# Order of the first loads, of the Gates' first products and of the background steps in a one-core hybrid mLSTM and gating layer

## The chip, the core and the metric

The kernel runs on one core of one Trainium2 chip. The metric is the device time of one execution in microseconds (us), as the median of several runs. The engines are TensorE (PE in the profile; PEld is its weight load), VectorE (DVE), ScalarE (ACT), GpSimd (POOL) and the queue of SyncE (SP), which here issues all DMAs.

## The reference

One layer over 1024 latent tokens and 256 context tokens of width 1024, in float32. What matters here is the feed-forward part, which stands twice in the layer for the latent tokens and once for the context, and the conditioning, which gives each of its shifts, scales and gates:

```python
mods = jnp.split(jax.nn.silu(c) @ w_ada[layer] + b_ada[layer], N_MOD, axis=-1)
mods_c = jnp.split(jax.nn.silu(c_ctx)[None] @ w_ada[layer] + b_ada[layer], N_MOD, axis=-1)

def ffn_sublayer(h, shift, scale, gate, g, w_in, w_out):
    hn = modulate(rmsnorm(h, g), shift, scale)
    a, b = jnp.split(hn @ w_in, 2, axis=-1)
    y = (jax.nn.silu(a) * b) @ w_out
    return h + 0.5 * gate[:, None, :] * y
```

`w_in` is 1024 x 5632, `w_out` 2816 x 1024. Between the two feed-forward parts lie the projections, a bidirectional mLSTM scan and a spatial gating, which the change does not touch.

## The kernel before

**Arithmetic.** Matrices are multiplied in pairs of float32r pages: `split` (L144, L145) copies a page on ScalarE into its high part and subtracts it on VectorE for the low part; three matmuls (high x high, high x low, low x high) make one product of a 128 x 128 block with 512 columns. The large products use seven block products in place of eight, in the manner of Strassen and Winograd: weights and activations are first added and subtracted in blocks. These block products are numbered 1 to 7. Product 1 and 2 need only the first token half's pages (`fa`), 5 and 6 the pages `fb`, 7, 4 and 3 the pages `fc`.

**Stages, in order.** (1) Prologue: four quarters of the first two conditioning vectors, as matmuls of `w_ada` pages of 256 KB (`ada_pages`, `ada_mm`, L803; tiles `adapg`, `adr`), the context's sum of squares (`Norm.sq`, `rstd`, `bcast`) and its normalised pages `hnc` (`mod0`). (2) The context's first feed-forward product, `pa` and `pb`, with weights loaded by `Weights`. (3) `A.gate` and (4) `A.outp`: the latent tokens' feed-forward. (5) The context's output, the projections, the scan, the merge. (6) `B.gate` and `B.outp`, the second feed-forward part.

**A Gate.** `Gate` walks over 22 weight rows `f`, paired as `kp` and `kp + 11`, each with products 1 to 7 of twelve matmuls (L381). The order is a list, `steps`. The first three `f` (0, 11, 1), the head, go side by side: product 1 of all three, product 2 of all three, and so on in the order `HSEQ`; all other `f` go one by one in the order `SEQ` = (1, 6, 5, 7, 2, 4, 3). Weights are loaded, combined (`presum` and `load`, on GpSimd, L347 to L365) and split `depth` products ahead into pages of a ring; `depth` is 4 and becomes larger at the first product 3, when the stage's input is given back and the pool `rg` is opened in its place. Results come together in banks A (products 1 and 2), B (6, 7, 4) and C (5, 3), so that VectorE must have read bank B after product 6 (`u1`, L401) before product 7 may add to it, and again after product 7 (`y2`, L404) before product 4. The pool for small pages "t2" has 12 slots, "fx" 12 as well; the raw rows of the head (`rawh`, two for each `f`) and their sums (`s1s`, two halves in a page) lie in "fx", loaded ahead by `preload`; other rows come into four slots `rawq`.

**Factors.** The pages of the second token half's combinations are made while the Gate runs: `Factors.late` gives a list of small items (in `B.gate` after `rstd`, some empty items, `bcast`, and with a normalisation `inplace` for each page). They go into the queue `todo`; `pump`, called after each three matmuls or so, pays 512 of credit, and an item costs 512 unless it says otherwise. An item that is due is taken out at once (`while not F.ready(p)`).

**Background.** A generator computes three more conditioning vectors on VectorE: 25 steps each, of which step 24 and 25 (`ada_fin`) use a small PSUM bank and end in `mods` (L758). It takes one step at each `tick`: in `A.gate` at each fourth product after number 36, in `A.outp` after each row of products other than 4 and 7.

**Order on an engine.** The framework lays out each engine's instructions by its own model of time, with the program's order as the priority. An engine can thus start a later piece of work where an earlier one is not ready in that model; on the chip each engine then runs its list in order.

## Time and profile before

| | us |
|---|---|
| median of 3 runs (lowest, highest) | 2702.27 (2700.63, 2704.98) |
| the profiled execution | 2708.92 |
| its span, first to last instruction | 2707.1 |
| TensorE busy | 2660.7 |
| VectorE busy | 1966.9 |
| ScalarE busy | 1081.5 |
| GpSimd busy | 447.6 |

The profile is of one execution. "Busy" counts each engine's own instructions; matmuls are pipelined and their ends are modelled, so that a matmul row lasts 0.39 us though the next one may start 0.23 us after it. Rows in order of time begin with start and duration; brackets at their end hold the idle time just before and what ended it. Rows by group hold the count, the busy time in us and the mean in ns.

### The profile page before, as it was taken

Reading aid. Unit: us, or ns where it says so; the run is one execution under the profiler, and the core shown is the slowest. Engines: PE = TensorE matmul, PEld = TensorE weight load, DVE = VectorE, ACT = ScalarE, POOL = GpSimd, SP = SyncE. Lnnn points to the kernel's source line nnn. Section 1 sums busy time; section 2 is a strip of 40 time slices with the busy share of each in tenths; the row PEclk is TensorE's granted clock in tenths of the full one; section 3 lists DMA queues with packets and bytes.
Section 4 is the critical chain, followed back from the end, with each engine's and each line's share of the span. In section 5 each row is a group of like instructions: output and inputs, shape, how many; then the busy total and the mean of one; then the engine's idle time right before and its main releaser. Section 6 shows DMA issues by size and latency. Waiting matters only on the chain.

```text
span 2707.1 us, 35713 instructions
## 1 busy us (share of the span) xinstructions
PE 2660.7 (98%) x12754; PEld 2211.7 (82%) x12754; DVE 1966.9 (73%) x3379; ACT 1081.5 (40%) x1840; POOL 447.6 (17%) x422
## 2 busy tenths in 40 slices
PE   9999999999999999999999999999999999999998
PEld 5987888887889878888888888888887788888887
DVE  4898777777979647788774878677568766666755
ACT  4663333334337525554443342112255333333432
POOL 0042323210000120000002005442102332320000
PEclk9999999999999999999999999999999999999999
DMA  8843344448588322246653477548140333337555
GB/s 297 309 172 117 121 152 140 137 163 309 186 262 273 110 78 85 105 142 215 192 164 113 142 236 260 168 164 283 57 158 20 130 138 124 106 125 262 201 159 171
DMA packets 202401, 456.74 MB, mean 169 GB/s; under 512 B 20592, under 2 KB 54640, under 8 KB 202224
## 3 DMA queue, kind: packets, MB, share of 16 engines
q1 hardware_dynamic: 202224, 454.47, 49.8%
q8 instruction: 100, 1.64, 0.3%
q14 instruction: 77, 0.63, 0.1%
HBM read 328.95 MB, written 125.51 MB: 168 GB/s over the span
## 4 chain that ended last, share of the span: by engine, by line
PE 73%; DVE 14%; DMA 5%; issue 4%; ACT 2%; POOL 1%; SPq 1%; POOLq 0%; DVEq 0%; ACTq 0%
PE pq L1232 14%; PE qb L381 13%; PE po L500 12%; PE pt L1700 9%; PE qa L381 7%; PE pr L1151 6%; DVE ring L145 2%; PE pc L1022 2%; PE pn L1813 2%; PE pu L1540 2%; DVE adacc L743 1%; DMA adapg<-in_w_ada_dram 1%; PE pkc L1212 1%; DMA graw<-fsp 1%; ACT ring L144 1%
## 5 line engine op out<-in xcount | busy, mean ns | idle before, releaser
L144 ACT CAST ring<-rawq 128x512 fp32r<-128x512 f32 x432 | 266.5, 621 | 569.3 <-PE qb L381 186.3
L145 DVE TENSOR_TENSOR ring<-rawq,ring 128x512 fp32r<-128x512 f32 x432 | 317.1, 738 | 159.7 <-ACT ring L144 158.2
L500 PE MATMUL po<-gring,wring 128*128 128x512 f32 (+1 forms) x1896 | 426.2, 385 | 3.7 <-DVE mods L758 2.8
L500 PEld LDWEIGHTS po<-gring,wring 128*128 128x128 f32 x1896 | 349.2, 188 | 76.5 <-issue 4.7
L381 PE MATMUL qb<-fc,ring 128*128 128x512 f32 x1440 | 344.6, 393 | 10.9 <-DVE y L404 5.6
L381 PEld LDWEIGHTS qb<-fc,ring 128*128 128x128 f32 x1440 | 271.4, 189 | 73.8 <-DVE u L401 10.0
L381 PE MATMUL qa<-fa,ring 128*128 128x512 f32 x1056 | 253.9, 390 | 1.2 <-DVE ring L145 0.7
L381 PEld LDWEIGHTS qa<-fa,ring 128*128 128x128 f32 x1056 | 197.7, 188 | 43.4 <-ACT ring L144 1.2
L381 PE MATMUL qb<-fb,ring 128*128 128x512 f32 x984 | 229.8, 389 | 0.0
L381 PEld LDWEIGHTS qb<-fb,ring 128*128 128x128 f32 x984 | 184.6, 188 | 38.7 <-DVE fb L145 0.3
L1232 PE MATMUL pq<-fc,ring 128*128 128x512 f32 x864 | 212.8, 394 | 0.5 <-DVE py L1245 0.4
L1232 PEld LDWEIGHTS pq<-fc,ring 128*128 128x128 f32 x864 | 160.8, 188 | 35.8 <-DVE py L1245 1.9
L144 ACT CAST wring<-rw 128x512 fp32r<-128x512 f32 x154 | 96.0, 623 | 224.8 <-PE po L500 196.5
L1700 PE MATMUL pt<-yp,ring 128*128 128x512 f32 x768 | 184.2, 396 | 0.0
L1700 PEld LDWEIGHTS pt<-yp,ring 128*128 128x128 f32 x768 | 144.1, 188 | 29.3
L145 DVE TENSOR_TENSOR wring<-rw,wring 128x512 fp32r<-128x512 f32 x154 | 106.1, 689 | 76.6 <-ACT wring L144 76.4
L1232 PE MATMUL pq<-fa,ring 128*128 128x512 f32 x576 | 142.3, 395 | 0.0
L1232 PE MATMUL pq<-fb,ring 128*128 128x512 f32 x576 | 137.6, 393 | 0.0
L1232 PEld LDWEIGHTS pq<-fa,ring 128*128 128x128 f32 x576 | 108.4, 190 | 23.1 <-DVE ring L145 0.2
L1232 PEld LDWEIGHTS pq<-fb,ring 128*128 128x128 f32 x576 | 107.6, 188 | 22.8 <-PE pu L1581 0.4
L743 DVE SCALAR_TENSOR_TENSOR adacc<-adapg,sc,adacc 128x512 f32<-128x512 f32 x140 | 107.3, 783 | 16.6 <-DMA adapg<-in_w_ada_dram 15.7
L144 ACT CAST ring<-rawt 128x512 fp32r<-128x512 f32 x64 | 39.6, 621 | 183.9 <-PE pt L1700 178.2
(343 smaller groups left out, 4342.1 us busy)
## 6 DMA issues: line engine op xcount, KB each, us to landing
adapg<-in_w_ada_dram SPq DMA_DIRECT2D x144, 256.0 KB, 3.6
fsp<-fhl SPq DMA_DIRECT2D x66, 512.0 KB, 2.7
gring<-fsp SPq DMA_DIRECT2D x66, 512.0 KB, 3.8
raw<-in_w1i_dram SPq DMA_DIRECT2D x44, 512.0 KB, 5.9
graw<-fsp SPq DMA_DIRECT2D x88, 256.0 KB, 3.0
rawq<-in_w1i_dram SPq DMA_DIRECT2D x38, 512.0 KB, 4.0
rawq<-in_w2i_dram SPq DMA_DIRECT2D x38, 512.0 KB, 3.3
fsp<-x SPq DMA_DIRECT2D x66, 256.0 KB, 2.8
```

The lines of the kernel that those rows point to most:

```text
L144: S.copy(hl[:, 0, :], src)
L145: V.tensor_sub(hl[:, 1, :], src, hl[:, 0, :].bitcast(F32))
L381: T.matmul(pt, hl[:, x, sl], pages[p][k][:, y, :], start=first and i == 0, stop=i == 11, skip_group_check=not first)
L500: T.matmul(pt[:, cs], w[:, x, sl], g[:, y, cs], start=grp and kp == 0 and i == 0, stop=kp == NFP - 1 and i == 2, skip_group_check=not grp)
L743: eng.scalar_tensor_tensor(acc, pgt, sc2[:, q, k:k + 1], acc, ALU.mult, ALU.add)
L1022: T.matmul(pt, hl[d // 4][:, x, sl], g[:, y, :], start=f == 0 and d % 2 == 0 and i == 0, stop=f == NF - 1 and i == 2, skip_group_check=True)
L1151: T.matmul(self.pt[m], pg[:, x, sl], hl[:, y, :], start=first and k == 0 and i == 0, stop=k == 3 and i == 2, skip_group_check=not first)
L1212: T.matmul(self.cp[:, o:o + 256], hl[:, x, k * 128:(k + 1) * 128], hnc[kc][:, y, :], start=p == 1 and k == 0 and i == 0, stop=p in (2, 4) ...
L1232: T.matmul(pt, hl[:, x, k * 128:(k + 1) * 128], pg[k][:, y, :], start=first and k == 0 and i == 0, stop=k == 3 and i == 2, skip_group_chec ...
L1540: T.matmul(pu[:, 0:257], ksl[:, kt * 128:(kt + 1) * 128], wv, start=True, stop=True)
L1700: T.matmul(pt, hl[:, x, k * 128:(k + 1) * 128], pg[:, y, :], start=kh + k + i == 0, stop=kh == 1 and k == 3 and i == 2)
L1813: T.matmul(pn[:, 0:257], qi[:, c_, :], self.C[d][:, c_, :], start=False, stop=c_ == 1)
```

## The change

Three parts. The prologue loads the second quarter's `w_ada` pages ahead of the context, and the context in two DMAs of four pages instead of eight of one; the context's `rstd` moves into the middle of the third quarter's products. The Gate's head has four `f`: products 1 and 2 of the first pair, products 1 and 2 of the second pair, then 5, 6, 7, 4, 3 of the first pair side by side, then 6, 5, 7, 4, 3 of each of the second pair by itself. Only the first pair's raw rows and sums lie in "fx"; the second pair's come through `rawq` and a slot of "t2". Items of `todo` in the Gate cost 640 instead of 512, with two more empty ones before `bcast` in the second. The background takes a step at each third product after number 42 and none in the last four rows of product 2.

```diff
--- before.py
+++ after.py
@@ -148,6 +148,14 @@
 
     def nop():
         pass
+
+    def it(f, *args):
+        return lambda: f(*args)
+
+    def slow(fn, *args, cost=1024):
+        f = it(fn, *args)
+        f.cost = cost
+        todo.append(f)
 
     credit = [0]
 
@@ -312,7 +320,7 @@
             return res
 
     SEQ = (1, 6, 5, 7, 2, 4, 3)
-    HSEQ = (1, 2, 5, 6, 7, 4, 3)
+    HSEQ = (5, 6, 7, 4, 3)
 
     class Gate:
 
@@ -321,7 +329,10 @@
             self.name, self.raw, self.ring, self.depth, self.sums, self.pairs = name, raw, ring, depth, sums, pairs
             fs = [f for kp in range(pairs) for f in (kp, kp + pairs)]
             self.head = fs[:head]
-            self.steps = [(f, p) for p in HSEQ for f in self.head] + [(f, p) for f in fs[head:] for p in SEQ]
+            two = [self.head[o:o + 2] for o in range(0, head, 2)]
+            self.steps = [(f, p) for fs_ in two for p in (1, 2) for f in fs_] + [(f, p) for p in HSEQ for f in two[0]]
+            self.steps += [(f, p) for fs_ in two[1:] for f in fs_ for p in SEQ if p > 2]
+            self.steps += [(f, p) for f in fs[head:] for p in SEQ]
             self.order = deque(self.steps)
             self.ready = deque()
             self.held = 0
@@ -508,7 +519,7 @@
                     for m, pt in enumerate(pts):
                         tile_(pt, kp, m, w, g)
                     self.fill()
-                    if tick is not None and p not in (4, 7):
+                    if tick is not None and p not in (4, 7) and not (p == 2 and kp > 6):
                         tick()
                 for hx in range(halves if p == 3 else 0):
                     cs = slice(hx * 512 // halves, (hx + 1) * 512 // halves)
@@ -522,7 +533,7 @@
             last()
 
     HLP = (3, 5, 6)
-    HEAD = 3
+    HEAD = 4
     warm = cp.tile([128, 1], F32, name="warm")
 
     fx = pool("fx", side="right")
@@ -561,11 +572,11 @@
             self.q = None
 
         def head(self):
-            s1s = [fxpage("s1s", F32) for _ in range(2)]
-            s1v = deque(pg[:, i, :] for pg in s1s for i in range(2))
+            s1s = fxpage("s1s", F32)
+            s1v = deque(s1s[:, i, :] for i in range(2))
             self.q = Gate(self.w_in, lambda f: fxpage("rawh", F32, (128, 1024)), self.ring, 4,
-                          lambda n: s1v.popleft(), NFP, HEAD)
-            self.heads = [(f, i) for i in (0, 1) for f in self.q.head]
+                          lambda n: s1v.popleft() if s1v else t2(n), NFP, HEAD)
+            self.heads = [(f, i) for i in (0, 1) for f in self.q.head[:2]]
 
         def preload(self):
             if self.heads:
@@ -598,7 +609,8 @@
             q, F = self.q, self.F
             q.raw = lambda f: xpage("raw", "rawq")
             q.fill()
-            todo.extend(items)
+            for fn in items:
+                slow(fn, cost=640)
             for n, (f, p) in enumerate(q.steps):
                 while not F.ready(p):
                     todo.popleft()()
@@ -610,7 +622,7 @@
                     q.sums = lambda n: self.rg.tile([128, 512], F32, name=n, tag="sums", bufs=2)
                     q.mid = lambda: self.rg.tile([128, 512], F32, name="ft", tag="ft", bufs=1)
                 q.step(f, p, F.pages, self.store)
-                if tick is not None and n % 4 == 0 and n > 36:
+                if tick is not None and n % 3 == 0 and n > 42:
                     tick()
             flush()
 
@@ -797,9 +809,11 @@
             pages.append(pg)
         return pages
 
-    def ada_mm(pages):
+    def ada_mm(pages, mid=None):
         pr = sm_ps("adr")
         for k in range(NKT):
+            if k == 4 and mid is not None:
+                mid()
             T.matmul(pr[0:2, 0:2 * QW], sc2[:, :, k], pages[k // KP][:, k % KP].rearrange("p m c -> p (m c)"),
                      start=k == 0, stop=k == NKT - 1)
         return pr
@@ -827,9 +841,6 @@
     def half_gate(i, m, q):
         V.tensor_scalar(hgate[:, i, q, :], mods[:, m, q, :], 0.5, None, ALU.mult)
 
-    def it(f, *args):
-        return lambda: f(*args)
-
     gcsp = dr.tile([NFP, 2, 128, 2, 256], F32, name="gcsp")
     W = Weights([("w1i", f, 1024) for f in range(2 * NF)], "w1")
     A = Stage("1", "w1i", 3)
@@ -838,9 +849,9 @@
     hc = [hcp[d // 4][:, d % 4, :] for d in range(NKT)]
     pos = fxpage("pos", F32, (128, 320))
 
-    def load_c(hc):
-        for d in range(NKT):
-            nc.sync.dma_start(hc[d], a["cT"][d])
+    def load_c(hcp, n):
+        for i, pg in enumerate(hcp):
+            nc.sync.dma_start(pg, a["cT"][i * n:(i + 1) * n].rearrange("d p t -> p d t"))
 
     def add_pos(tb, d):
         hv = h[tb][d].rearrange("p (r c) -> p r c", c=64)
@@ -855,9 +866,9 @@
     for _ in range(10):
         T.matmul(junk[:, 0:128], ones, ones, start=True, stop=True)
     apg = [ada_pages(0)]
-    load_c(hc)
-    for qt in (1, 2, 3):
-        apg.append(ada_pages(qt))
+    apg.append(ada_pages(1))
+    load_c(hcp, 4)
+    apg += [ada_pages(2), ada_pages(3)]
     nc.sync.dma_start(cst[:, 1:], a["cst"].rearrange("p (a b) -> p a b", a=5)[:, 1:])
     nc.sync.dma_start(pos, a["pos"])
     hncp = [fxpage("hnc", F32R, (128, 2, 2, 256)) for _ in range(4)]
@@ -871,11 +882,10 @@
     for d in range(NKT):
         nct.sq(d)
     prs.append(ada_mm(apg[1]))
-    nct.rstd()
     for qt in range(NQ):
         ada_out(qt, prs[qt])
         if qt < 2:
-            prs.append(ada_mm(apg[qt + 2]))
+            prs.append(ada_mm(apg[qt + 2], None if qt else nct.rstd))
         if qt == 0:
             nct.bcast()
         if qt:
@@ -885,11 +895,6 @@
 
     n1 = [Norm(h[tb], 512, V) for tb in range(2)]
     s0, b0 = smod[:, 0, 0, :], mods[:, 0, 0, :]
-
-    def slow(fn, *args, cost=1024):
-        f = it(fn, *args)
-        f.cost = cost
-        todo.append(f)
 
     for f in range(NF):
         if f < NKT:
@@ -1009,7 +1014,7 @@
 
     hcp = [t2("hc", F32, (128, 2, 256)) for _ in range(4)]
     hc = [hcp[d // 2][:, d % 2, :] for d in range(NKT)]
-    load_c(hc)
+    load_c(hcp, 2)
     pcs = [mm_ps("pc") for _ in range(4)]
     wload(2)
     wsplit(1)
@@ -1956,7 +1961,7 @@
                     todo.append(lambda k=k, p=p: B.F.early(fpage, p, k))
     flush()
     n1_ = n3[1]
-    B.gate([n1_.rstd] + [nop] * 3 + [n1_.bcast] + B.F.late(fpage, lambda k: [lambda: n1_.inplace(k, m7, m6)]))
+    B.gate([n1_.rstd] + [nop] * 5 + [n1_.bcast] + B.F.late(fpage, lambda k: [lambda: n1_.inplace(k, m7, m6)]))
 
     def put(n_, tb, d, pool_, cs=slice(0, 512)):
         o_ = n_.h[d]
```

## The prediction

> **What bounds the kernel now.** I read the page first, then the waits of TensorE, then its order of time in the places that the waits name, then VectorE in the same stretches.
>
> ```profile
> span 2707.1 us, 35713 instructions
> PE 2660.7 (98%) x12754; PEld 2211.7 (82%) x12754; DVE 1966.9 (73%) x3379; ACT 1081.5 (40%) x1840; POOL 447.6 (17%) x422
> ...
> PE qb L381 <- DVE y L404: 5.6, 4, 2.7
> PE qb L381 <- DVE u L401: 5.4, 11, 2.4
> PE qa L381 <- DVE u L401: 4.0, 2, 2.6
> PE adr L803 <- DMA adapg<-in_w_ada_dram: 3.8, 3, 2.4
> PE rb L215 <- DVE diag L211: 2.9, 2, 1.8
> PE po L500 <- DVE mods L758: 2.8, 2, 2.3
> ```
>
> TensorE is busy for 98% of the span, so only its idle time can be won, 46.4 us in all by this row, and a little more that hides in slow matmuls. The waits (total, times, longest) lie where the change works: the Gate's products (L381, three rows, 15.0 us), the first products of the prologue (L803) and the first output stage (L500). Not one matmul is added or removed.
>
> The second Gate, in TensorE's order of time (start, duration, then in brackets the idle time and its releaser):
>
> ```profile
> 2041.69 2.43 PE L381 MATMUL qa<-fa,ring 128*128 128x512 f32 x10
> ...
> 2049.11 1.10 PE L215 MATMUL rb<-diag,ones 128*128 128x512 f32 x2 [1.11 <-DVE diag L211]
> ...
> 2079.57 3.00 PE L381 MATMUL qa<-fc,ring 128*128 128x512 f32 x12 [1.47 <-DVE u L401]
> 2085.14 15.51 PE L381 MATMUL qa<-fc,ring 128*128 128x512 f32 x60 [2.57 <-DVE u L401]
> 2100.49 8.32 PE L381 MATMUL qb<-fc,ring 128*128 128x512 f32 x36
> 2108.65 2.88 PE L381 MATMUL qa<-fa,ring 128*128 128x512 f32 x12
> ...
> 2116.81 0.61 PE L381 MATMUL qa<-fa,ring 128*128 128x512 f32 x2
> 2119.82 4.61 PE L381 MATMUL qb<-fc,ring 128*128 128x512 f32 x12 [2.39 <-DVE u L401]
> ...
> 2126.55 5.60 PE L381 MATMUL qb<-fc,ring 128*128 128x512 f32 x24
> ```
>
> 36 matmuls from 2100.49 to 2108.65 are three products: 2.72 us for a product of twelve. The head's 21 products should take 57.1 and take 2108.65 - 2041.69 = 67.0: 9.8 lost, of which about 1.5 are the Norm's own small matmuls (`rb` at 2049.11 and the sums ahead of it). The next five products (13.6) take 17.9: 4.3 lost. After the two longest waits matmuls run slowly: 60 took 15.51 where 13.8 is due, 12 took 4.61 where 2.9 is. A long wait costs about 1.7 on top of itself. So 12.6 us can be won here.
>
> The reason is VectorE (a window with busy us of PE, PEld, DVE, ACT, POOL; the groups of that window; its order of time, with GpSimd's):
>
> ```profile
> 2050.00:2109.00 59.00, 54.96 (x233) 44.38 (x232) 56.48 (x84) 33.55 (x56) 11.13 (x6) 0.97 0.04 14
> ...
> L293 DVE TENSOR_TENSOR h<-h 128x512 f32<-128x512 f32 x16 | 13.1, 852 | 0.0
> L145 DVE TENSOR_TENSOR fc<-h,fc 128x512 fp32r<-128x512 f32 x12 | 8.7, 729 | 0.0
> L246 DVE SCALAR_TENSOR_TENSOR h<-h,smod,rb 128x512 f32<-128x512 f32 x8 | 5.8, 742 | 1.3 <-PE rb L215 1.3
> ...
> 2080.43 3.46 DVE L293 TENSOR_TENSOR h<-h 128x512 f32<-128x512 f32 x2
> 2084.41 0.68 DVE L401 TENSOR_TENSOR u<-p,qa 128x512 f32<-128x512 f32 x1
> 2085.01 0.68 DVE L145 TENSOR_TENSOR ring<-rawh,ring 128x512 fp32r<-128x512 f32 x1
> ...
> 2079.92 3.42 POOL L348 TENSOR_TENSOR rawq<-rawq 128x512 f32<-128x512 f32 x2
> ```
>
> It is busy for 56.5 of 59 us. Operations start 0.60 apart (2084.41, 2085.01). The product at 2085.14 starts when the `u` add of 2084.41 is done, and that add stood behind two subtractions that took 3.46, not some 1.3, while GpSimd worked on 2079.92 to 2083.34.
>
> **The change part by part.**
>
> *Heads of the Gates.* Twelve products of different data now run ahead of product 7, as before, but eight of them (not six) need only the pages that stand since the start. The dues, counted in products from the head's start, go for product 5, 6, 7, 4, 3 from 6, 9, 12, 15, 18 to 8, 10, 12, 14, 16. VectorE's work for these pages: 8 `inplace` (some 0.66 apart), 16 subtractions, 20 splits, 5.3 + 36 x 0.60 = 26.9, from 2050 on. Up to product 7: 19.7 of it, nine ring splits 5.4, two `u` adds 1.2 (three before): 26.3, with 2 lost to GpSimd ends at 2078.3; TensorE is there at 2041.7 + 32.6 + 2 = 2076.3. Wait: 2.0. Then two products (5.4) against pages of product 4 (4.8), two ring splits (1.2), three adds (1.8): 2.4 more. Then 5.4 against 2.4 + 1.2 + 3.6: 1.8 more. What helps beyond this count is room: s1s and rawh take 5 of 12 "fx" slots and not 8, so the pages of products 4 and 3 need not wait for raw rows to be used up. After the first pair ten products (27.2) stand against ten ring splits, fourteen adds, eight operations of `out`: 32 x 0.60 = 19.2, covered; without that cover the next wait is the fifth matrix's first product, whose banks free last. Left: 6.2 and something for the adjacency below, 6.6 of 12.6. **Gain 6.0**, ends -3 and 12.6.
>
> The third and fourth matrix's GpSimd sums (two operations each) move into the gate; GpSimd's two at 2079.92 cost VectorE 3.46 - 1.3 = 2.1. That is in the 2 us above; at the worst, both on the path, 2 x 2.1. [...]
>
> *Product 4 right behind product 7* in the second pair: product 4 accumulates in the bank that the `y` add (L404) must read first; elsewhere product 2 stands between. Two places in each Gate. Bounds: nothing, if TensorE takes other work (at 2116.81 it started two matmuls of product 2 ahead of product 7, so the order on the engine is filled by what is ready); 0.68 for the add and some 0.2 each way when VectorE is free; 2.7, the longest wait in the row on `y`, when it isn't. Queued behind it: all later products. I take 0.9 for each, half of them filled: 0.4 in the second Gate (above) and 0.9 in the first.
>
> *First Gate.* Same order, without `inplace`:
>
> ```profile
> 239.25 2.88 PE L381 MATMUL qa<-fa,ring 128*128 128x512 f32 x12
> ...
> 255.68 7.38 PE L381 MATMUL qb<-fc,ring 128*128 128x512 f32 x24 [2.67 <-DVE y L404]
> 262.89 2.88 PE L381 MATMUL qa<-fa,ring 128*128 128x512 f32 x12
> ...
> 283.19 2.88 PE L381 MATMUL qa<-fa,ring 128*128 128x512 f32 x12
> ...
> 239.00:263.00 24.00, 21.33 (x87) 17.15 (x86) 22.33 (x33) 8.89 (x16) 8.75 (x5) 0.93 0.53 168
> ```
>
> Seven products from 239.25 to 262.89: 23.6 for 19.0, 4.6 lost; seven more to 283.19: 20.3, 1.3 lost. VectorE is busy 22.33 of 24 there, with what three matrices that end together leave behind. Two and two spread this. I take 1.2 left and 0.9 for the adjacency: **gain 3.8**, ends -3 (all four waits as long as the row's) and 5.9.
>
> The Gate's item rate (cost 640 for 512) puts one item on 1.25 slots: 51 items are done by slot 64, product 16; product 3's page is due just there, so the rate itself adds nothing while VectorE is the bound. The two more empty items let `bcast` fall later than `diag`; the wait on `diag` in the second head (1.11) is inside the 12.6.
>
> *Background.* It advances every third product from 45 and not every fourth from 40: 37 steps for 29. Each is two operations:
>
> ```profile
> L743 DVE SCALAR_TENSOR_TENSOR adacc<-adapg,sc,adacc 128x512 f32<-128x512 f32 x140 | 107.3, 783 | 16.6 <-DMA adapg<-in_w_ada_dram 15.7
> ```
>
> 8 x 2 x 0.78 = 12.5 us of VectorE move into the Gate, over 109 products, some 300 us; VectorE waits there for these pages' DMA, with the adds that TensorE needs queued behind. Ends 0 and 3; **loss 0.5**.
>
> The first output stage, where it leaves off:
>
> ```profile
> 674.90 0.94 PE L500 MATMUL po<-gring,wring 128*128 128x512 f32 x3 [0.49 <-DVE mods L758]
> 678.14 2.08 PE L500 MATMUL po<-gring,wring 128*128 128x512 f32 x8 [2.30 <-DVE mods L758]
> ```
>
> Product 4's banks wait for the read of `ada_fin`'s small banks. The generator's step 49/50 falls on output step 20/21 before (the 9th and 10th row of product 2), on 12/13 after (its 1st and 2nd), and no step stands in rows 7 to 10: the reads are done some nine rows, 24 us, ahead. **Gain 2.8**, ends 0 and 2.8.
>
> *Prologue.*
>
> ```profile
> 5.69 5.98 SPq L843 DMA_DIRECT2D hc<-in_cT_dram  x8
> ...
> 15.05 1.88 PE L803 MATMUL adr<-adapg,sc 128*2 128x512 f32 x4 [2.41 <-DMA adapg<-in_w_ada_dram]
> 17.97 5.31 PE L803 MATMUL adr<-adapg,sc 128*2 128x512 f32 x12 [1.04 <-DMA adapg<-in_w_ada_dram]
> ...
> 24.73 7.03 PE L803 MATMUL adr<-adapg,sc 128*2 128x512 f32 x16
> ...
> 41.23 1.69 PE L170 MATMUL pa<-hnc,hl 128*128 128x256 f32 x12
> ...
> 24.00:28.00 4.00, 4.00 (x16) 1.39 (x16) 2.45 (x17) 0.00 (x0) 0.00 (x0) 1.00 1.09 348
> ...
> 37.34 1.05 ACT L144 CAST hl<-raw 128x1024 fp32r<-128x1024 f32 x1 [0.24 <-DMA raw<-in_w1i_dram]
> ```
>
> Eight issues of context (1 MB, 5.98 us of SP's queue) stand ahead of the second quarter, whose products wait 2.41 and 1.04. Moved behind it as two issues, the second group can follow the first at 15.05 - 2.41 = 12.6 and end at 12.6 + 7.0 = 19.7 in place of 23.3: 3.6 earlier. But the DMA engines are full (348 GB/s, share 1.09), so 1 MB is 3.0 us and a page of two rows 1.5: the second quarter's first page lands at 15.05 - 3.0 = 12.0, its last at 16.5, the context at 19.5, the third quarter's first page at 21.0. The third group then ends near 21.0 + 7.0 + 0.5 (the sums of `rstd` now in its middle) = 28.6, not 31.8. `rstd` needs the context's eight squares, which fit between 19.5 and the group's middle, 24.5. Two quarters on, the first weights decide: the second one's cast waits for its DMA at 37.34, the same bytes lie ahead of it as before, and with 1.05 for the cast and some 1.2 for the subtraction it is ready at 39.6; the products cannot run on before that, where they start at 41.23 now. **Gain 1.6**, ends 0 and 3.6.
>
> **Sum**: 6.0 + 3.8 - 0.5 + 2.8 + 1.6 = 13.7. The profiled execution took 2708.92 (span 2707.1, 1.8 around it): 2695.2 in its place. It lies 6.65 above the median of the runs, 2702.27, and the difference carries over: **2688.6**.
>
> [...]
>
> **The rivals.**
>
> 1. *The waits only move.* VectorE has the same work in the second head, and 56.5 of 59 us are taken. Dues of products 4 and 3 come earlier by 1 and 2 products. Then both heads keep their losses and only the prologue and the output stage win: 4.4 less 0.5, 2698. For it: the busy share. Against it: a quarter of the lost time is slow matmuls, and room for pages was part of the delay.
>
> 2. *Slower: product 4 waits behind product 7* at all four places with VectorE behindhand: 2.7 and the slow stretch 1.7 each, 17.6. It decides if the `y` add stands more than about 2.4 behind the product. With the heads' gain at half (4.9) and 3.9 for the rest: 2702.3 + 17.6 - 8.8 = 2711. For it: the longest wait today is on just this add, with a product between. Against it: fill at 2116.81, and VectorE's load falls to 19 of 27 there.
>
> 3. *All of it goes*: 12.6 + 5.9 + 2.8 + 1.6 = 22.9, 2679. Against it: the count above leaves VectorE late by 6.
>
> 4. *The loads don't do what they say*: the prologue is bound by bytes and wins nothing; 2690 with the rest. It lies inside the forecast.
>
> **How the numbers follow.** A measurement here can tell some 0.2%, 5.4 us, from no change. Forecast (2681 to 2696, with rival 4) 0.52; rival 1 0.20, of which 0.04 lies below 2696.9; rival 2 0.18; rival 3 0.08; slower by something I have not named 0.02. Faster 0.52 + 0.08 + 0.04 = 0.64, within 0.16, slower 0.20. Likeliest 2688.6. The range 2677 to 2710 leaves out half of rival 2 and what lies below 2677.
>
> **What would show it.** The second head: TensorE from its first `qa` to the end of the fourth matrix, 28 products, 76.2 us if nothing is lost; I expect 84. The two waits on L401 of 2.4 and more gone. The first Gate: no wait above 1.5 on L404 before its tenth matrix. Output: no wait on L758. Prologue: `adr` without a wait in its second group, with one in the third, the first `pa` at 39.6. Wrong is the forecast if L404 waits stand four times above 2, or if VectorE stays full and the lost time reappears at products 4 and 3.

## The result and the profile after

The changed kernel takes 2710.12 us (median of 9 runs, 2707.45 to 2713.85); the kernel before, run beside it, 2703.44 (9 runs, 2700.63 to 2706.38). The ratio is 1.0024, with a 95% interval of 1.0016 to 1.0033: slower by 0.16 to 0.33%. The forecast was 2688.6, faster, with a range of 2677 to 2710.

The profile's page of the changed kernel, its first lines, and from its waits of TensorE the longest (total, times, longest):

```profile
span 2712.1 us, 35689 instructions
PE 2664.1 (98%) x12754; PEld 2212.5 (82%) x12754; DVE 1975.7 (73%) x3379; ACT 1080.7 (40%) x1840; POOL 433.6 (16%) x422
...
PE qa L392 <- DVE y L415: 8.4, 5, 4.9
PE qa L392 <- ACT ring L144: 5.1, 4, 2.3
PE qb L392 <- DVE y L415: 4.0, 3, 1.9
PE qb L392 <- DVE u L412: 3.0, 8, 1.7
...
PE adc L826 <- ACT adrow L823: 2.3, 1, 2.3
```

L392, L412, L415 and L422 are L381, L401, L404 and the multiply of product 4 in the kernel before. The waits on the `u` add of 5.4 and 4.0 have shrunk to 3.0 and one of 1.9; a new one has come, on ScalarE's part of the weight pages (`ring`, L144), and the one on `y` has grown from 5.6 to 12.4. So the waits named ahead did go, and others replaced them.

Where they lie is seen from the length of the stages. The table is worked out from the first matmul of each stage in the traces, one execution each. "First 345" is the time from a Gate's first product matmul to its 346th, so the heads and a little behind them; at the pace of the undisturbed products, 2.72 us for twelve, it would be 78.2. The rows add up to the span.

| us | before | changed |
|---|---|---|
| start to the first `pa` | 41.2 | 41.8 |
| first `pa` to the first Gate | 139.7 | 140.0 |
| first Gate (its first 345) | 431.2 (84.1) | 435.8 (87.4) |
| first output stage | 217.4 | 214.3 |
| from there to the second Gate | 1212.2 | 1208.6 |
| second Gate (its first 345) | 437.1 (92.3) | 442.9 (97.8) |
| second output stage | 228.4 | 228.6 |

Both Gates lost, 4.6 and 5.9, and 3.3 and 5.5 of that in the first 345 matmuls. The stretch between the first output stage and the second Gate is no gain of the change: in the thirteen other profiles of this document it takes 1206.1 to 1210.6, and only in this one of the kernel before 1212.2. The second Gate in TensorE's order of time:

```profile
2040.49 2.43 PE L392 MATMUL qa<-fa,ring 128*128 128x512 f32 x10
...
2075.41 5.87 PE L392 MATMUL qa<-fc,ring 128*128 128x512 f32 x24
2081.97 1.63 PE L392 MATMUL qa<-fc,ring 128*128 128x512 f32 x6 [0.69 <-DVE y L415]
2084.28 2.11 PE L392 MATMUL qa<-fc,ring 128*128 128x512 f32 x8 [0.68 <-DVE y L415]
2086.69 2.56 PE L392 MATMUL qa<-fc,ring 128*128 128x512 f32 x10 [0.29 <-DVE fc L145]
2089.09 5.60 PE L392 MATMUL qb<-fc,ring 128*128 128x512 f32 x24
2097.03 0.73 PE L392 MATMUL qa<-fb,ring 128*128 128x512 f32 x2 [2.34 <-ACT ring L144]
2098.62 4.12 PE L392 MATMUL qa<-fb,ring 128*128 128x512 f32 x10 [0.86 <-DVE ring L145]
...
2108.09 0.74 PE L392 MATMUL qa<-fb,ring 128*128 128x512 f32 x2 [1.68 <-ACT ring L144]
...
2119.32 4.46 PE L392 MATMUL qa<-fc,ring 128*128 128x512 f32 x12 [4.92 <-DVE y L415]
```

Up to 2094.5 all went better than forecast: product 7 starts at 2075.4 (2076.3 plus a wait of 2.0 was counted), and the first pair's last ten products lose 0.69, 0.68 and 0.29. Then TensorE stands for 2.34 and 0.86 for the converted weights of the third matrix, for 1.68 for the fourth's, and for 4.92 for an add. GpSimd's order of time shows why the weights are late:

```profile
2042.24 1.71 POOL L376 TENSOR_TENSOR rawh<-rawh 128x512 f32<-128x512 f32 x1 [1.44 <-DVE ring L145]
2090.50 1.67 POOL L358 TENSOR_TENSOR s<-rawq 128x512 f32<-128x512 f32 x1 [46.54 <-DVE x L422]
2092.24 1.62 POOL L359 TENSOR_TENSOR rawq<-rawq 128x512 f32<-128x512 f32 x1
2093.83 1.27 POOL L358 TENSOR_TENSOR s<-rawq 128x512 f32<-128x512 f32 x1
...
2101.47 1.62 POOL L376 TENSOR_TENSOR rawq<-rawq 128x512 f32<-128x512 f32 x1
2109.49 1.29 POOL L358 TENSOR_TENSOR s<-rawq 128x512 f32<-128x512 f32 x1 [6.40 <-DMA rawq<-in_w2i_dram]
...
2113.20 1.58 POOL L374 TENSOR_TENSOR rawq<-s,rawq 128x512 f32<-128x512 f32 x1 [0.72 <-DVE ring L145]
2114.74 1.71 POOL L358 TENSOR_TENSOR s<-rawq 128x512 f32<-128x512 f32 x1
2116.53 1.59 POOL L359 TENSOR_TENSOR rawq<-rawq 128x512 f32<-128x512 f32 x1
```

The first sum of the third matrix (`presum`, L358) waits 46.5 us, and not for its weights: for the multiply of product 4 of the first pair (L422). That multiply is the last reader of a `p1`, and so gives back a slot of "t2". By the code the pool's 12 slots are full at that place: four matrices hold `p1` and `x1` (products 1 and 2 of all four are done), which is 8, and the first pair `u1` and `y2`, which is 4. The `s1` of the third matrix would be the 13th. (The fourth matrix's `s1` is asked for only after the pool `rg` has opened, and comes from there; in this Gate it stands behind the third's in GpSimd's list.) So eight GpSimd operations run in one piece from 2090.50 to 2103.1, when their results are already due. VectorE is slowed beside them, and again beside GpSimd's next operations, from 2109.49 on:

```profile
2097.01 1.56 DVE L145 TENSOR_TENSOR ring<-rawq,ring 128x512 fp32r<-128x512 f32 x1
2098.49 1.77 DVE L145 TENSOR_TENSOR ring<-s,ring 128x512 fp32r<-128x512 f32 x1
...
2104.17 0.68 DVE L427 TENSOR_TENSOR u<-u,y 128x512 f32<-128x512 f32 x1
...
2113.56 1.77 DVE L145 TENSOR_TENSOR fhl<-u,fhl 128x512 fp32r<-128x512 f32 x1
2115.25 1.75 DVE L145 TENSOR_TENSOR fhl<-x,fhl 128x512 fp32r<-128x512 f32 x1
2116.92 1.74 DVE L441 TENSOR_TENSOR x<-x,ft 128x512 f32<-128x512 f32 x1
2118.59 0.68 DVE L415 TENSOR_TENSOR y<-p,qa 128x512 f32<-128x512 f32 x1
```

An operation of this shape takes 0.68 at 2104.17, while GpSimd is idle (2103.09 to 2109.49), and 1.56 to 1.77 while GpSimd works.

The `y` add at 2118.59, which TensorE waits 4.92 for, stands behind three such operations. GpSimd's work beside these three is not the second pair's, but the sums of the next two matrices. Their raw rows need the four slots `rawq` that the second pair's rows had held, and SyncE's queue asks for them from 2103.70 on, when its late sums are over. So this wait follows from the late sums only at one remove; no run tests that link by itself.

### The profile page after: what moved, and what is told of

Same layout as the page of the kernel before. It is cut to its first block, busy times and chain, and to the rows that moved or that the text cites. A ratio compares the mean times of both kernels' runs of the same rounds, so it can differ in the third digit from the quotient of the medians.

```text
span 2712.1 us, 35689 instructions
## 1 busy us (share of the span) xinstructions
PE 2664.1 (98%) x12754; PEld 2212.5 (82%) x12754; DVE 1975.7 (73%) x3379; ACT 1080.7 (40%) x1840; POOL 433.6 (16%) x422
## 4 chain that ended last, share of the span: by engine, by line
PE 79%; DVE 9%; issue 6%; DMA 3%; ACT 1%; POOL 1%; SPq 0%; POOLq 0%; DVEq 0%; ACTq 0%
PE pq L1237 15%; PE po L511 14%; PE qb L392 14%; PE pt L1705 9%; PE qa L392 6%; PE pr L1156 6%; PE pc L1027 2%; DVE ring L145 2%; PE pa L178 2%; PE pb L178 2%; PE pn L1818 1%; PE pu L1545 1%; DVE adacc L755 1%; PE pkc L1217 1%; PE pn L1816 1%
## 5 line engine op out<-in xcount | busy, mean ns | idle before, releaser
L144 ACT CAST ring<-rawq 128x512 fp32r<-128x512 f32 x444 | 273.6, 620 | 591.1 <-PE qb L392 179.8
L145 DVE TENSOR_TENSOR ring<-rawq,ring 128x512 fp32r<-128x512 f32 x444 | 333.7, 755 | 158.9 <-ACT ring L144 157.0
L392 PE MATMUL qb<-fc,ring 128*128 128x512 f32 x1392 | 330.4, 390 | 7.8 <-DVE y L415 4.0
L392 PEld LDWEIGHTS qb<-fc,ring 128*128 128x128 f32 x1392 | 260.2, 188 | 66.8 <-DVE u L412 6.4
L392 PE MATMUL qa<-fa,ring 128*128 128x512 f32 x1056 | 253.1, 390 | 0.7 <-ACT ring L144 0.5
L392 PEld LDWEIGHTS qa<-fa,ring 128*128 128x128 f32 x1056 | 197.9, 188 | 42.9 <-ACT ring L144 0.9
L392 PE MATMUL qb<-fb,ring 128*128 128x512 f32 x960 | 224.6, 389 | 0.0
L392 PEld LDWEIGHTS qb<-fb,ring 128*128 128x128 f32 x960 | 180.2, 188 | 37.5
L144 ACT CAST wring<-rw 128x512 fp32r<-128x512 f32 x154 | 95.9, 623 | 215.3 <-PE po L511 201.3
L1705 PEld LDWEIGHTS pt<-yp,ring 128*128 128x128 f32 x768 | 144.1, 188 | 29.3
L144 ACT CAST ring<-rawt 128x512 fp32r<-128x512 f32 x64 | 39.7, 620 | 187.1 <-PE pt L1705 180.1
```

Of the source, the lines that this page charges most:

```text
L144: S.copy(hl[:, 0, :], src)
L145: V.tensor_sub(hl[:, 1, :], src, hl[:, 0, :].bitcast(F32))
L392: T.matmul(pt, hl[:, x, sl], pages[p][k][:, y, :], start=first and i == 0, stop=i == 11, skip_group_check=not first)
L1705: T.matmul(pt, hl[:, x, k * 128:(k + 1) * 128], pg[:, y, :], start=kh + k + i == 0, stop=kh == 1 and k == 3 and i == 2)
```

## The experiments

Times are medians; ratios are to the kernel before, run beside each on the same chip (its medians there: 2704.09, 2703.73, 2703.54 and 2703.06 us). The Gates are of one execution each. How far that can be trusted is seen from kernels with the same heads: the first 345 take 84.1 to 85.3 and 90.5 to 92.3 in the kernel before, e1_prologue, e3_ticks and e4_rate, and 87.4 and 97.8 to 98.0 in the changed kernel and e8_copyv.

| | time | ratio (95%) | first Gate (345) | second Gate (345) |
|---|---|---|---|---|
| e1_prologue | 2704.95 | 1.000 (0.999, 1.001) | 430.6 (84.2) | 435.4 (90.5) |
| e2_heads | 2709.27 | 1.002 (1.001, 1.003) | 437.1 (89.8) | 441.8 (96.8) |
| e3_ticks | 2705.01 | 1.0003 (0.9994, 1.0013) | 432.7 (84.1) | 437.1 (92.3) |
| e4_rate | 2702.31 | 0.9997 (0.9988, 1.0005) | 435.0 (85.3) | 436.8 (91.6) |
| e5_side | 2713.17 | 1.0041 (1.0029, 1.0053) | 438.9 (87.8) | 438.9 (93.5) |
| e6_nosums | 2696.54 | 0.9975 (0.9966, 0.9985) | 430.8 (82.5) | 432.7 (88.1) |
| e8_copyv | 2712.07 | 1.0030 (1.0017, 1.0043) | 437.2 (87.4) | 443.2 (98.0) |
| e9_p2back | 2699.92 | 0.9982 (0.9974, 0.9991) | 431.4 (80.3) | 434.0 (89.3) |
| e10_p2early | 2701.80 | 0.9996 (0.9987, 1.0004) | 433.0 (84.2) | 434.0 (89.3) |
| e11_hold | 2710.16 | 1.0026 (1.0015, 1.0037) | 433.6 (84.0) | 440.5 (96.0) |
| e12_heads9 | 2698.94 | 0.9988 (0.9979, 0.9997) | 427.1 (80.5) | 440.9 (96.3) |
| e13_headrate | 2696.41 | 0.9975 (0.9966, 0.9984) | 427.7 (80.9) | 433.9 (89.4) |

### One part alone

Each of the four is the kernel before with one part of the diff: the loads of the context, quarters and `rstd`; the heads; the background's steps; the items' cost.

```diff
@@ e1_prologue
+    apg.append(ada_pages(1))
+    load_c(hcp, 4)
@@ e2_heads
+    HEAD = 4
@@ e3_ticks
+                if tick is not None and n % 3 == 0 and n > 42:
@@ e4_rate
+                g_.cost = 640
```

The other lines of each part are as in the diff of the change; e4_rate gives each item its cost in a line of its own.

> The kernel before with the prologue's part alone (second quarter ahead of the context, context in two DMAs, rstd inside the third quarter). Theory P: ScalarE's list has the context's squares ahead of the copy of the first quarter's row, so with the context later that copy comes later too; the first pa starts near 41.8 as in the changed kernel (41.2 before), and the time is 0 to 1.5 us above before. Rival (the prediction's): the part wins 1.6 us by itself, first pa near 39.6.

> The kernel before with the Gate's head part alone (four matrices, two and two, second pair's rows through rawq and t2), items at 512, background as before. Theory H: this part carries the loss, some +5 us in each Gate, +8 to +12 us in all, with waits of TensorE on ring pages and on the y add between the first pair's product 3 and the third matrix's product 4. Rival R: the head is harmless by itself and the changed rates of items and background make the waits; then within 2 us of before.

> The kernel before with the background's part alone (a step at each third product from 45, none in rows 7 to 10 of product 2). Theory H: the wait on ada_fin's banks in the first output stage goes (2.8 us) and the first Gate stays within 1 us: 2.5 to 3.5 us faster than before. Rival R: the closer steps load VectorE in the first Gate and give the 2.8 us back or more: 0 to +3 us.

> The kernel before with the item rate alone (640 for 512, five empty items instead of three before bcast in the second Gate). Theory H: nothing that can be measured, within 1.5 us of before, the wait on diag in the second head gone or smaller. Rival R: the slower rate makes the pages late in the second head: +2 to +5 us.

The heads alone carry the loss: the time is 5.2 us above the kernel before (8 to 12 had been expected), and the Gates take 437.1 and 441.8, beside 435.8 and 442.9 in the changed kernel. The other three parts, each by itself, can't be told from no change. For e3_ticks that is a miss: 2.5 to 3.5 us had been expected from the waits on L758, which are gone there, and the time is no shorter. In e1_prologue the first `pa` starts at 42.2, as its theory P said, and not near 39.6.

### The second pair's five products side by side

```diff
-  self.steps += [(f, p) for fs_ in two[1:] for f in fs_ for p in SEQ if p > 2]
+  self.steps += [(f, p) for fs_ in two[1:] for p in SEQ if p > 2 for f in fs_]
```

> The changed kernel with the second pair's five products side by side too, so that the fourth matrix's product 7 stands between the third's product 7 and product 4. Theory Y (the adjacency: product 4 stands right behind the y add): the waits on y of 4.9, 1.1 and 1.0 go, the second Gate falls from 442.9 to some 437 and the first from 435.8 to some 433. Theory S (the second pair's GpSimd sums come late, because s1 needs a t2 slot that the first pair's product 4 gives back, and they block VectorE): the fourth matrix's sums are now due one product after the third's, waits on ring pages grow by some 2 us, the second Gate stays at 441 or more.

Another matrix's product now stands between 7 and 4. The second Gate is 4.0 shorter than in the changed kernel, the first 3.1 longer, and the whole is no better: neither theory's numbers came. The waits on `y` did not go, 11.4 us in all against 12.4. In the second Gate TensorE waits 1.52 and 2.60 for `ring`, on ScalarE's part: side by side, the late sums of both matrices are wanted at once. So a product between 7 and 4 does not by itself remove the loss.

### The second pair's sums left out

This kernel leaves out GpSimd's sums for the second pair in both Gates and multiplies by the raw weights in their place. The products after one another in a matrix stay as in the changed kernel.

```diff
+            elif f in self.head[2:]:
+                a1, a2 = self.half(f, 0)
+                b1, b2 = self.half(f, 1)
+                src = {6: a1, 5: b2, 7: b1, 4: b2, 3: a2}[p]
```

> The changed kernel without the second pair's GpSimd sums in both Gates: its products 6, 5, 7, 4, 3 take raw rows (so its outputs are other numbers); eight of GpSimd's operations less in each Gate, all else as in the change. Theory S: the ring waits (2.3, 0.9, 1.7 in the second Gate, 1.1 in the first) go and VectorE's operations of 1.77 between 2098 and 2104 fall to 0.69; the second Gate falls from 442.9 to 436 or less, and the first by 2 to 4. Theory Y: the waits on y stay as they are, the second Gate stays at 440 or more.

2696.54: 13.6 less than the changed kernel. The first Gate is 5.0 shorter and the second 10.3; the waits on `ring` are gone, and of the waits on an add behind the first pair 1.93 and 1.10 are left in the first head, 2.31 in the second. It shows that the sums cost the time, not yet why: without them GpSimd also runs nothing beside VectorE there (in the second Gate it is idle for 57.70, until 2095.68).

### The prologue's copies on VectorE

In the prologue of the changed kernel the second pass is as forecast: ScalarE's order of time, and TensorE's:

```profile
18.68 0.42 ACT L201 ACTIVATE acc<-hc 128x256 f32<-128x256 f32 x1 [14.40 <-DMA hc<-in_cT_dram]
19.00 1.01 ACT L204 ACTIVATE sq<-hc 128x256 f32<-128x256 f32 x3
20.18 1.33 ACT L204 ACTIVATE sq<-hc 128x256 f32<-128x256 f32 x4 [0.16 <-DMA hc<-in_cT_dram]
21.42 1.03 ACT L823 COPY adrow<-adr 2x512 f32<-2x512 f32 x2
...
7.56 12.18 PE L817 MATMUL adr<-adapg,sc 128*2 128x512 f32 x28
22.03 1.05 PE L826 MATMUL adc<-cst,adrow 2*128 2x2 f32 x8 [2.29 <-ACT adrow L823]
23.01 5.29 PE L817 MATMUL adr<-adapg,sc 128*2 128x512 f32 x8
...
41.84 1.69 PE L178 MATMUL pa<-hnc,hl 128*128 128x256 f32 x12
```

The second quarter runs without a wait and ends at 19.7. But ScalarE's list has the squares of the context, which now lands later, ahead of the copy that TensorE needs next. The first quarter's matmuls are over at 12.87, ScalarE then stands idle for the context until 18.68, and the copy comes behind the squares, at 21.42: 2.29 us of idle for TensorE, and then eight products in 5.29 where the next eight take 3.60. This kernel copies on VectorE instead.

```diff
-        S.copy(row, pr[0:2, 0:2 * QW])
+        V.tensor_copy(row, pr[0:2, 0:2 * QW])
```

> The changed kernel with the prologue's four small row copies (adrow) on VectorE and not on ScalarE. Theory P (ScalarE's list keeps the first copy behind the context's squares): the 2.3 us wait of adc on adrow goes, the first adc starts near 19.9 and not 22.0, the first pa near 39.8 to 40.5 and not 41.8. Rival: the bytes decide, adr of the third quarter waits for its pages in place of adrow, and pa stays at 41.5 or later.

VectorE's list, too, has the copy behind the squares' adds; TensorE waits 2.98 for it, and `pa` starts at 45.86, 4.0 later. It is the place in the list, not the engine. More telling is what follows: the first Gate starts at 182.35, 0.5 later than the changed kernel's 181.80. The first context stage takes up the rest, so that a gain at `pa` would hardly have come through either. Neither theory's start of `pa` came.

### Product 2 of the second pair back in its old place

```diff
-  self.steps = [(f, p) for fs_ in two for p in (1, 2) for f in fs_] + [(f, p) for p in HSEQ for f in two[0]]
-  self.steps += [(f, p) for fs_ in two[1:] for f in fs_ for p in SEQ if p > 2]
+  self.steps = [(f, p) for p in (1, 2) for f in two[0]] + [(f, 1) for f in self.head[2:]] + [(f, p) for p in HSEQ for f in two[0]]
+  self.steps += [(f, p) for f in self.head[2:] for p in SEQ[1:]]
```

> The changed kernel with product 2 of the second pair put back between its products 7 and 4 (order 1; then 6, 5, 7, 2, 4, 3), so that six products and not eight run ahead of product 5, no y add stands right ahead of its product, and two t2 slots less are taken when s1 of the third matrix is asked for. Theory Y or S: both Gates lose their waits behind the first pair, the second Gate 437 or less. Theory D (VectorE is behindhand, whatever the order): the lost time moves back to products 5 to 7 of the first pair, which now fall due 5.4 us earlier; the second Gate 440 or more.

Two products fewer stand ahead, and `x1` of the second pair is taken only later: 10 slots of "t2" are held and two are free for the sums. GpSimd's order of time in the second Gate:

```profile
2040.67 1.29 POOL L358 TENSOR_TENSOR s<-rawq 128x512 f32<-128x512 f32 x1
2042.04 1.30 POOL L359 TENSOR_TENSOR rawq<-rawq 128x512 f32<-128x512 f32 x1
...
2045.35 1.29 POOL L358 TENSOR_TENSOR s<-rawq 128x512 f32<-128x512 f32 x1
```

Counted from the Gate's start, the sums run some 46 us earlier, with no wait. Behind the first pair TensorE waits once, 1.15 for `y`. Both Gates shorten by 4.3 and 8.9 against the changed kernel, and the time falls below the kernel before.

### The same order, with the slots held

e9_p2back puts product 2 between 7 and 4 as well, so it doesn't separate the slots from the order. This kernel keeps its order and only takes the slot early:

```diff
                 S.copy(u["p1"], pt)
+                if f in self.head[2:]:
+                    u["x1"] = t2("x1")
+                    S.copy(u["x1"], pt)
```

> The order of e9_p2back (product 2 of the second pair back between its products 7 and 4), but the second pair takes its x tile from t2 already at product 1, as in the changed kernel: two slots are held from there on (one ScalarE copy into each is added, about 0.6 us, four in the program, beside waits for nothing). Theory S (the sums come late because the t2 slots have run out): GpSimd's first sum of the second pair waits for the multiply of line 422 again, as in the changed kernel (46.5 us there in the second Gate), the sums run in one piece behind it, and the Gates go from 431.4 and 434.0 back to 435 to 437 and 439 to 443 us; the time is 2706 to 2712, the ratio 1.001 to 1.003. Rival N (what cost was eight products ahead instead of six, or product 2's place by itself): both Gates stay within 1.5 of 431.4 and 434.0, and the time at 2698 to 2702.

GpSimd's first sum of the second pair, and TensorE behind the first pair:

```profile
2088.99 1.67 POOL L358 TENSOR_TENSOR s<-rawq 128x512 f32<-128x512 f32 x1 [44.71 <-DVE x L426]
...
2095.53 0.73 PE L392 MATMUL qa<-fb,ring 128*128 128x512 f32 x2 [2.34 <-ACT ring L144]
...
2107.28 4.61 PE L392 MATMUL qa<-fc,ring 128*128 128x512 f32 x12 [2.84 <-DVE u L415]
```

The wait of the sum is back, and with it the same 2.34 for `ring`, 440.5 us for the second Gate and 2710.16 in all: with the order unchanged, holding two slots costs 10.2 us against e9_p2back (the added copies, four in the program, are some 0.6 each on ScalarE, an estimate from the changed kernel's copies of this shape, 0.58 in the mean of 44 at L409). The first Gate went up by only 2.2 (435 to 437 had been expected, 433.6 came). Of what the first 345 lose between e9_p2back and the changed kernel, 7.1 and 8.5, the slots bring back 3.7 in the first Gate and 6.7 in the second. The rest goes with the order of the products, in the first Gate nearly half; no run shows by which wait.

### Sums called earlier still

e9_p2back with `presum` called where product 1 of the second pair is loaded.

```diff
+                if p == 1 and f in self.head[2:]:
+                    self.presum(f)
```

> e9_p2back, with GpSimd's first two sums of each matrix of the second pair called when its product 1 is loaded, ahead of the first pair's products. In e9_p2back they ran at 2040 to 2048 us already, so theory S expects no more than the last wait in front of the second pair to go (1.15 us in the second Gate, for the add of y): both Gates within 1.5 of 431.4 and 434.0, 2698 to 2701. [...]

The second Gate is unchanged to 0.1. The first has one wait of 2.93 on `y`, followed by slow matmuls (twelve in 4.57), where e9_p2back has 1.23 on `x`; its first 345 take 3.8 more and the whole Gate 1.6. The time misses the expected range by 0.8 and shows nothing to win.

### The heads of e9_p2back alone, and with the rate

The first of these two kernels is the kernel before with the heads alone.

```diff
+  self.steps = [(f, p) for p in (1, 2) for f in two[0]] + [(f, 1) for f in self.head[2:]] + [(f, p) for p in HSEQ for f in two[0]]
```

> The kernel before with the heads of e9_p2back alone: no other loads of the context, no other background, the items of the second Gate at their old cost. If the other three parts are worth nothing (each was within 0.1% alone), the Gates stand as in e9_p2back (431.4 and 434.0, within 2) and the time is 2698 to 2702, the ratio 0.998 to 0.999. Rival: the other parts only pay once the heads run freely (the background takes TensorE's time from the converted products that the head no longer lacks); then the second Gate is at 436 or more and the time 2702 to 2704, no other than the kernel before.

The time came as expected, 2698.94, but by luck: neither Gate did, the first is 4.4 shorter than in e9_p2back, the second 6.9 longer. The rival had the second Gate right, and the time not. TensorE in the second Gate:

```profile
2038.38 1.36 PE L215 MATMUL rb<-diag,ones 128*128 128x512 f32 x2 [3.45 <-DVE diag L211]
...
2066.16 10.39 PE L384 MATMUL qa<-fc,ring 128*128 128x512 f32 x36 [2.79 <-DVE u L404]
```

At the old rate `bcast` is called too early for its `diag` (3.45): 22 product matmuls stand ahead of it here and 39 in e9_p2back. The `u` add comes late (2.79); that the denser items cause it is a reading, which the next kernel tests. The last kernel adds the rate, and leaves the old background:

```diff
+                g_.cost = 640
...
+    B.gate([n1_.rstd] + [nop] * 5 + [n1_.bcast] + B.F.late(fpage, lambda k: [lambda: n1_.inplace(k, m7, m6)]))
```

> The kernel before with the heads of e9_p2back and the second Gate's item rate (cost 640, five empty items), with the old background and the old loads of the context. In e12_heads9 the first Gate took 427.1 us (431.4 in e9_p2back, which has the new background), the second 440.9 (434.0 in e9_p2back, which has the new rate), where TensorE waited 3.45 for diag and 2.79 for an add of u. Theory R (the two parts that seemed worth nothing alone do count once the heads run freely: the rate gains in the second Gate, the background loses in the first): first Gate 426 to 429, second 433 to 436, the time 2690 to 2695, the ratio 0.995 to 0.997. Rival: the 4 us of the first Gate and the 7 us of the second are differences between single executions, and no part but the heads counts; then the time is that of e9_p2back and e12_heads9, 2698 to 2701.

Both Gates came as theory R said, 427.7 and 433.9, with `rb` waiting for nothing and a longest wait of 1.15 in the second head:

```profile
2042.04 1.02 PE L215 MATMUL rb<-diag,ones 128*128 128x512 f32 x2
...
2065.70 6.01 PE L384 MATMUL qa<-fc,ring 128*128 128x512 f32 x24 [0.61 <-DVE u L404]
...
2098.14 3.00 PE L384 MATMUL qa<-fc,ring 128*128 128x512 f32 x12 [1.15 <-DVE y L407]
```

The time, 2696.41, is 1.4 above the expected range: against e12_heads9 the Gates took 6.3 less in the profiled executions, and the other stages, whose code is the same, 3.1 more. At 0.9975 (0.9966 to 0.9984) it is the fastest of the kernels that compute the whole layer. Between it, e9_p2back and e12_heads9 the intervals overlap; the stage lengths carry the reading, not the ratios.

A "t2" of more slots, which would be the direct test, was not run.

## Why the prediction was wrong

**The step that failed** is the one on the second pair: "After the first pair ten products (27.2) stand against ten ring splits, fourteen adds, eight operations of `out`: 32 x 0.60 = 19.2, covered", together with "The third and fourth matrix's GpSimd sums (two operations each) move into the gate ... at the worst, both on the path, 2 x 2.1". I had counted the room in "fx", which the change makes, and not in "t2", which it takes. With all 12 slots held, the third matrix's sum couldn't be taken early. Eight operations, four for each matrix and not two, came late, one behind the other, and the next two matrices' sums came late behind them; beside both, VectorE's operations stretched to 1.75. TensorE waits 2.34 + 0.86 + 1.68 for the second pair's pages and 4.92 for the `y` add, 9.8 in all, and runs slowly behind the longer ones (ten matmuls in 4.12 from 2098.62 on and twelve in 4.46 from 2119.32 on, at a granted clock of 0.59 and 0.65). The windows ahead of the end of the first pair and behind it (busy us of PE, PEld, DVE, ACT, POOL; granted clock; DMA):

```profile
2050.00:2094.50 44.50, 42.83 (x183) 33.31 (x181) 41.96 (x67) 27.32 (x47) 3.92 (x3) 1.00 0.04 13
2094.50:2124.00 29.50, 19.70 (x69) 14.75 (x69) 26.53 (x28) 10.36 (x19) 16.26 (x11) 0.88 0.40 137
```

**Point by point.**

- *First pair of the second head.* Right in mechanism, and under-rated: 2.0 + 2.4 + 1.8 were left by the count, waits of 1.66 in all came. The two waits of 2.57 and 2.39 on L401 are gone.
- *Second pair.* Wrong, as above; e6_nosums, e9_p2back and e11_hold show it. The second Gate was to win 6.0 and lost 5.9; its first 28 products, forecast at 84, took 95.9 (90.5 before).
- *First Gate.* Gain of 3.8 forecast, loss of 4.6. The same cause, in part. GpSimd's waits of the changed kernel show one such sum in each Gate (46.5 and 29.3):

```profile
POOL s L358 <- DVE x L422: 75.8, 2, 46.5
```

  In the first Gate three of the eight operations had run early and only five came late. The slow product behind 240.59, which is quoted in the last section, comes just after them. By e11_hold the slots make up some half of the distance between this head and that of e9_p2back. With free slots and the old background (e13_headrate) the first Gate wins 3.5 against the profile before. That this is close to the forecast says little for its sum, since product 2 stands elsewhere there.
- *Product 4 right behind product 7*, rival 2. Its 2711 lies beside the result by luck. It asked for waits of 2.7 at all four places; one of 4.92 came, and 1.03 and 1.10 in the first Gate. With the two products still adjacent and the sums left out the second Gate took 432.7; apart and with the slots held, 440.5. There adjacency is at most a small part; in the first Gate its share is open. The 0.2 each way between the two engines was an estimate that no row shows: in the second Gate of the changed kernel two products start 0.14 and 0.05 after the ends of their `y` adds (2081.83 and 2081.97, 2084.23 and 2084.28).
- *Rate.* "The rate itself adds nothing while VectorE is the bound" held with the old heads (e4_rate) and not with heads that run freely: from e12_heads9 to e13_headrate, which has the rate and the two more empty items, the second Gate falls by 6.9.
- *Background.* 0.5 was put too low: with the new steps the first Gate has waits of 1.80 and 1.89 on `y` where before it had one of 1.75, and from e9_p2back to e13_headrate, which has the old ones, it falls by 3.7. Single executions spread here: behind its first 345 matmuls the first Gate takes 346.4 to 349.7 in the six profiles with the old steps and 348.3 to 351.1 in the eight with the new. The means lie 2.2 apart, which is the better estimate of the loss.
- *Output stage.* The waits on L758 are gone, as forecast, but that was no gain of 2.8: in the six profiles with the old steps they range from 0.3 to 2.8 (0.5 and 0.3 in e1_prologue and e4_rate), and the stage takes 213.4 to 217.4; in the eight with the new ones there is no such wait, and it takes 212.8 to 216.4. The 2.8 is the highest of the six and belonged in part to the profiled execution, which lay 6.65 above the median; the sum took that difference off and the wait once more.
- *Prologue.* The loads do what they say, the second quarter doesn't wait. Third group and `pa` were forecast at 28.6 and 39.6; they came at 32.4 and 41.8, since the copy behind the squares in ScalarE's list was not counted. e8_copyv shows that `pa` 4 us later costs 0.5 at the first Gate, so the term was near nothing in either case: rival 4's outcome, for another reason.
- *Signs.* Several that were to show the forecast came although it failed: no wait above 1.5 on `y` before the first Gate's tenth matrix, none on L758, none in the second quarter. In the second Gate the lost time reappeared at products 6 and 4 of the second pair, and not at 4 and 3 of the first, where the prediction looked for it.

## What to carry to other kernels

When a step is moved ahead, count every pool that it holds something in up to its new place, the small ones too, and ask who takes the next slot: here the freed pool was not the one that ran out. Work that is off the critical path but comes from a shared pool can be held back until it is due all at once; here, run in one piece, it also slowed another engine, whose operations of 0.68 took 1.56 to 1.77 beside it. Parts that measure nothing alone should be tried again once the main stall is gone, and a wait seen in a single profile should be seen in a second one before it is counted as a gain.

## What the runs showed of the hardware

In these runs TensorE's products after a wait went at one of two paces, and the length of the wait didn't settle which. In the first Gate of the changed kernel, two waits of nearly the same length:

```profile
240.59 4.51 PE L392 MATMUL qa<-fc,ring 128*128 128x512 f32 x12 [1.87 <-DVE u L412]
...
516.52 3.01 PE L392 MATMUL qb<-fc,ring 128*128 128x512 f32 x12 [1.89 <-DVE y L415]
```

Twelve matmuls took 4.51 after the one and 3.01 after the other; the granted clock over them was 0.62 and 1.00. Counted over the fourteen profiles (waits of TensorE of 1.4 us and more, behind the prologue, with twelve matmuls of 128x512 behind them that nothing interrupts): of 25 waits up to 1.80 us none was followed by the slow pace, of 24 from 1.81 to 2.39 thirteen were, of 17 from 2.51 up fifteen. The two exceptions lasted 3.01 and 3.29. In all the slow cases the granted clock over the twelve was 0.50 to 0.67, in all the others 1.00. A wait of 1.81 was enough once (in the first Gate of e9_p2back, twelve matmuls in 4.60 behind it); what decides in a single case stays open.
